# Six places of a decoder layer's schedule moved: fold order, x loads, pool factors, rotary tables, splits behind a copy, an early Exp

## The chip, the cores and the metric

The kernel runs on one core of one Trainium2 chip. The core has TensorE (PE, matmuls into PSUM banks), VectorE (DVE), ScalarE (ACT), GpSimd (POOL) and SyncE (SP, which here only issues transfers), and 16 DMA engines that all transfer queues share. The metric is device time in microseconds (us) of one launch. About 0.2% of it, 4.9 us, is what a measurement of this kernel can tell from no change.

## The reference

One decoder layer in fp32: 2048 tokens, 1024 columns. It is a mixer (retention with rotary tables and a pooling branch, one output projection), cross-attention into 256 memory tokens, and a gated MLP with a short convolution, with a residual after each and a final RMSNorm.

```python
h = rmsnorm(x, mix_norm_g)
q, k, v, gate, u = split(h @ w_in)
mix = concat(head_rmsnorm(retention(rope(q), rope(k), v)) * silu(gate), pool_mixer(u, pool_w, pool_scale))
x = x + mix @ w_out
mem_n = rmsnorm(mem, mem_norm_g)
x = x + cross_attn(rmsnorm(x, xa_norm_g), mem_n, wq, wkv, wo)     # 4 heads, softmax over 256 memory tokens
x = x + conv_glu_ffn(rmsnorm(x, ffn_norm_g), w_up, conv_w, conv_b, w_down)
return rmsnorm(x, final_norm_g)
```

## The kernel before

Every fp32 matmul is made of three passes over pairs. `split` makes a pair: ACT copies the high half (L257, or L260 with a scale), DVE subtracts it from the source to get the low half (L241, or L249 with a scale). `passes` then issues high x high, high x low and low x high (L269, L270, L271). So every operand costs ACT and DVE work ahead of PE, and a low half that is late holds PE at L270 or L271.

**Order.** The engines' instruction orders are made when the kernel is built: a scheduler goes through the program and gives each instruction a place on its engine, with the program's order as priority. `tc.keep_in_program_order` pins an instruction to the program's order on its engine, and `tc.issue_after(x)` keeps instructions behind another. Each engine then runs its list strictly in order: what waits holds all that is behind it.

**Stages.** (1) Start-up, to about 123 us, folds weights: `folded_weights` runs a list of units, K (memory keys, eight), V (memory values, eight), M (score weights: `wq` times keys, evacuated at L552), O (output weights: values times `wo`, L567), W (pool weights: pool factors times `wout_p`, L591). K 1 also starts the memory's norm (sums on PE at L374, copy at L379); odd K units split a pair of keys that the M units need. Between units the caller loads eight tiles of x (`load_x_wide`): a transfer, a scaled split (L260 on ACT, L249 on DVE), a square (L631 on ACT) and an add on DVE (L241), all pinned in order. The list `x_at` tells behind which units. The first W unit also loads the pool factors `poolT`, scales them on DVE and splits them. (2) The value projections, to about 168 us. (3) `head_projections` for the first half of the tokens (b = 0): query, key, gate and pool groups in pairs, each pair as seven block products instead of eight, with sums of blocks made beforehand. Each product fills one PSUM bank; `evac` copies it out (L1668) or adds it, and `final` applies the rotary tables (L1684 on ACT). The tables come back from `rope_d` by four transfers (L1582) and are scaled on DVE in `scaled_tables`, one of the steps that `step()` advances. `settle()` makes the pairs of finished results for the output projection. (4) Output projection and residual, (5) cross-attention from about 455 us on: per tile of 128 tokens a score product, a row maximum on DVE (L893), an Exp on ACT (L897), a transpose on PE (L870). (6) Stages 2 to 5 again for the second half (b = 1, to about 1195 us), and (7) the MLP to the end.

**Weight sums.** Beside stages 2 to 5 POOL makes the sums of weight blocks in HBM (`weight_sums`): copies and accumulating transfers into `Ad`, `Ud` and `Dd`. Its pace is set by tokens: the program calls `next(under[0])` at fixed places, and every `spacing[0]`-th call writes a token on ACT (`halo`, L957) that POOL copies (L958) before it issues that step's transfers (L938, L941). During start-up's last units spacing is 2, in the values 1, in the heads 3 and 7.

The lines that set the order of start-up:

```python
x_at = (2, 4, 6, 8, 10, 12, 18, 19)
for n, _ in enumerate(folded_weights()):
    if n in x_at:
        load_x_wide(x_at.index(n), total)
```

Of the kernel before, what the change touches and what calls it, by code (L numbers as in the profile page):

```python
# [12 lines left out]
ALU = mybir.AluOpType  # L13
# [123 lines left out]
def trunk(ctx, tc, xT, memT, pos, w_qkgu, w_v, wkv, wqT, wo, wout_r, wout_p, poolT, w_up, w_dn, vecs, consts, outT):  # L137
# [285 lines left out]
    def folded_weights():  # L423
# [147 lines left out]

        pool_pair = []

        def pool_weights(g):

            if g == 0:
                raw = new_raw()
                r3 = raw[:, :SUB].rearrange("p (g c) -> p g c", g=4)
                sp.dma_start(r3, poolT.rearrange("g p c -> p g c"))
                pw = prs.take()  # L580
                tt(dve, r3, r3, bcast(pscale, P), ALU.mult)
                split(raw[:, :SUB], pw.r[:, :SUB], pw.r[:, SUB:])
                pool_pair.append(pw)
            pw = pool_pair[0]
            u = row_pair(wout_p[g])
            for nh in range(2):
                ps = mmps()
                lh = [pw.r[:, i * SUB + g * P : i * SUB + (g + 1) * P] for i in range(2)]
                passes(ps, lh, [r[:, nh * SUB : (nh + 1) * SUB] for r in u], True, True)
                t = result()  # L590
                act.activation(t.f, ps, AF.Copy)  # L591
                keep(tiles4(WPd, nh, g), t, 4)
            if g == 3:
                pw.free()
# [4 lines left out]
                r.free()  # L599

        K, V, M, O, W = keys, memory_values, score_weights, output_weights, pool_weights
        for f, *a in ((K, 0), (K, 1), (K, 2), (K, 3), (K, 4), (K, 5), (K, 6), (M, 0), (K, 7), (V, 0), (M, 1), (V, 1), (V, 2), (M, 2),
                      (V, 3), (V, 4), (O, 0), (M, 3), (V, 5), (O, 1), (V, 6), (V, 7), (O, 2), (W, 0), (W, 1), (O, 3), (W, 2), (W, 3),
                      (none_left,)):
            f(*a)
            yield


# [233 lines left out]
    def attention(sums, beside, pace):  # L842
# [31 lines left out]
            e.free()  # L874

        turned.clear()
        mw = [[], []]
        for _ in load_m(0):
            pass
# [674 lines left out]
    def head_projections(b, v, rb, t1, t2, z, got):  # L1554
# [7 lines left out]
        prs.freed.append(len(prs.one))  # L1562
        prs.one.append(Arena(new_s(F32R, 0), 0, 1, T))
        chained.clear()
        todo, ready, mix, gates, outs, tables = [], [], [None] * KT, {}, {}, []

        def place():
# [9 lines left out]
        def scaled_tables():  # L1577
            out = Z.take(2)
            tables.append(out)
            for to, half in ((0, 0), (0, 1), (2, 0), (1, 1)):  # L1580
                p, i = slice(64 * half, 64 * half + 64), min(to, 1)
                sp.dma_start(out.f[p, i * T : (i + 1) * T].rearrange("p (s c) -> p s c", s=NS), rope_d[to].rearrange("(s p) c -> p s c", s=NS))  # L1582
            yield
            yield
            for j in range(KT // 2):
                negated(part_of(z, 1, j), *xpair(j, 1))
                yield
            z.free(2, 2)
            for i in range(2):
                for s in range(NS):  # L1590
                    d = out.f[:, i * T + s * SUB : i * T + (s + 1) * SUB]
                    tt(dve, d, d, rb[s].f[:, :SUB], ALU.mult)
                yield
# [37 lines left out]
        class Heads(Member):  # L1631
# [26 lines left out]
            def evac(self, i, ps):  # L1658
                role, q = ((0, 0), (1, 1), (0, 1), (0, 0), (1, 1), (0, 1), (1, 0))[i]
                d = self.acc[role][q]  # L1660
                if (role, q) == (1, 0):
                    self.final(role, q, d, ps)
                elif (role, q) in self.seen:
                    tt(dve, d, d, ps, ALU.subtract if role else ALU.add)
                    self.final(role, q, d, d)
                else:
                    self.seen.add((role, q))
                    act.activation(d, ps, AF.Copy, scale=-1.0 if role else 1.0)  # L1668

            def final(self, role, q, d, src):  # L1670

# [8 lines left out]
                if kind < 2:  # L1680
                    cs, cols = tables[0], slice(q * SUB, (q + 1) * SUB)
                    c, sn = cs.f[:, cols], cs.f[:, T + q * SUB : T + (q + 1) * SUB]
                    for to, at in ((slice(0, 64), slice(64, 128)), (slice(64, 128), slice(0, 64))):
                        act.activation(side[to], src[at], AF.Copy, scale=1.0 if src is d else -1.0)  # L1684
# [108 lines left out]
        for at, (m, i) in enumerate(items[:own]):  # L1793
# [7 lines left out]
                passes(ps, [pr[:, h, j * P : (j + 1) * P] for h in range(2)], operand(i, j), j == 0 and i in (0, 1, 3), j == KT // 2 - 1, i != 3)  # L1801
            made[at].free()
            m.evac(i, ps)
            fill()
            if at == own - 3:
                for _ in range(5):
# [18 lines left out]
        while todo:  # L1825
            step()
# [105 lines left out]
    for b in range(NB):  # L1932
# [261 lines left out]
```

## Time and profile before

| | |
|---|---|
| median of 3 runs | 2435.37 us (2433.79 to 2436.63) |
| profiled execution | 2434.47 us, span 2432.7 us, mean TensorE clock 0.993 |
| PE busy | 2398.6 us, 99% of the span |
| DVE, ACT, POOL busy | 1737.0, 1347.0, 304.7 us |
| DMA queues' share of 16 engines | q1 49.7%, q0 (POOL's accumulating transfers) 14.7%, q10 3.3% |

A row of the timeline gives start, duration, engine, line, operation and tiles, and in brackets the idle time of the engine before it with what ended it. Names such as `Z`, `R`, `G`, `Q` are buffers that many tiles share. A matmul's duration includes its pipeline; back to back they start 0.227 us apart (128 x 512). A window of a stage has a granted clock of its own, 1.00 in most of the span.

### The profile page before, as it was taken

Reading aid. Unit: us, or ns where it says so; the run is one execution under the profiler, and the core shown is the slowest. Engines: PE = TensorE matmul, PEld = TensorE weight load, DVE = VectorE, ACT = ScalarE, POOL = GpSimd, SP = SyncE. Lnnn points to the kernel's source line nnn. Section 1 sums busy time; section 2 is a strip of 40 time slices with the busy share of each in tenths; the row PEclk is TensorE's granted clock in tenths of the full one; section 3 lists DMA queues with packets and bytes.
Section 4 is the critical chain, followed back from the end, with each engine's and each line's share of the span. In section 5 each row is a group of like instructions: output and inputs, shape, how many; then the busy total and the mean of one; then the engine's idle time right before and its main releaser. Section 6 shows DMA issues by size and latency. Waiting matters only on the chain.

```text
span 2432.7 us, 33367 instructions
## 1 busy us (share of the span) xinstructions
PE 2398.6 (99%) x11232; PEld 2003.4 (82%) x11232; DVE 1737.0 (71%) x2869; ACT 1347.0 (55%) x2457; POOL 304.7 (13%) x484
## 2 busy tenths in 40 slices
PE   8999999999999999999999999999999999999998
PEld 8877888788888888888888888888888888888887
DVE  8646776565767675565788776887677698867875
ACT  7744553344545453334655655765555577666663
POOL 0045554543000000000001010020000000000000
PEclk9999999999999999999999999999999999999999
DMA  8999999989542234375567564755556478758951
GB/s 311 329 290 289 287 284 301 283 215 308 165 116 83 70 120 142 101 285 168 180 211 260 188 203 147 251 191 164 174 156 212 126 241 308 242 185 277 350 176 73
DMA packets 272844, 514.67 MB, mean 212 GB/s; under 512 B 29856, under 2 KB 60960, under 8 KB 272672
## 3 DMA queue, kind: packets, MB, share of 16 engines
q1 hardware_dynamic: 210640, 398.11, 49.7%
q0 software_dynamic: 37376, 86.00, 14.7%
q10 hardware_dynamic: 24656, 28.43, 3.3%
q8 instruction: 88, 1.44, 0.2%
q14 instruction: 84, 0.69, 0.1%
HBM read 410.19 MB, written 188.22 MB: 246 GB/s over the span
## 4 chain that ended last, share of the span: by engine, by line
PE 89%; DMA 4%; DVE 4%; issue 2%; ACT 2%; SPq 0%; DVEq 0%; ACTq 0%
PE mm L269 28%; PE mm L270 27%; PE mm L271 27%; DVE Z L241 1%; PE aux L269 1%; PE aux L271 1%; PE aux L270 1%; PE aux L870 1%; PE aux L777 1%; PE aux L762 1%; DVE Z L249 1%; DMA Z<-rope_d 1%; PE aux L779 1%; PE aux L751 1%; DVE T L241 1%
## 5 line engine op out<-in xcount | busy, mean ns | idle before, releaser
L269 PE MATMUL mm<-G,Q 128*128 128x512 f32 (+1 forms) x1570 | 610.2, 390 | 5.4 <-ACT T L1668 3.0
L271 PE MATMUL mm<-G,Q 128*128 128x512 f32 (+1 forms) x1570 | 608.0, 389 | 6.2 <-DVE Q L241 6.2
L270 PE MATMUL mm<-G,Q 128*128 128x512 f32 (+1 forms) x1442 | 560.4, 389 | 0.2 <-DVE G L249 0.2
L269 PE MATMUL mm<-G,E 128*128 128x512 f32 (+1 forms) x1132 | 430.2, 383 | 2.2 <-ACT G L257 2.0
L270 PE MATMUL mm<-G,E 128*128 128x512 f32 (+1 forms) x1132 | 431.6, 381 | 0.0
L271 PE MATMUL mm<-G,E 128*128 128x512 f32 (+1 forms) x1132 | 429.2, 382 | 1.2 <-DVE E L241 1.2
L269 PEld LDWEIGHTS mm<-G,Q 128*128 128x128 f32 x1570 | 296.3, 189 | 67.3 <-ACT T L1668 3.4
L271 PEld LDWEIGHTS mm<-G,Q 128*128 128x128 f32 x1570 | 296.4, 189 | 66.2 <-DVE Q L241 6.8
L270 PEld LDWEIGHTS mm<-G,Q 128*128 128x128 f32 x1442 | 272.2, 189 | 54.3 <-DVE G L249 0.4
L241 DVE TENSOR_TENSOR Z<-Z,mm 128x512 f32<-128x512 f32 (+1 forms) x322 | 216.3, 676 | 123.3 <-PE mm L271 117.8
L249 DVE SCALAR_TENSOR_TENSOR Z<-Z,vecs 128x1024 f32<-128x1024 f32 x176 | 224.9, 1282 | 50.3 <-ACT Z L1106 47.0
L269 PEld LDWEIGHTS mm<-G,E 128*128 128x128 f32 x1132 | 213.0, 188 | 43.6 <-ACT G L257 2.2
L271 PEld LDWEIGHTS mm<-G,E 128*128 128x128 f32 x1132 | 212.6, 188 | 42.6 <-DVE E L241 1.6
L270 PEld LDWEIGHTS mm<-G,E 128*128 128x128 f32 x1132 | 212.8, 188 | 41.1
L1043 ACT ACTIVATE E<-R 128x512 fp32r<-128x512 f32 (+1 forms) x165 | 101.5, 615 | 140.9 <-PE mm L270 134.9
L241 DVE TENSOR_TENSOR Q<-R,Q 128x512 fp32r<-128x512 f32 (+1 forms) x153 | 106.1, 695 | 65.8 <-ACT Q L257 37.0
L241 DVE TENSOR_TENSOR T<-T 128x512 f32<-128x512 f32 (+4 forms) x196 | 134.7, 692 | 19.9 <-ACT T L416 10.9
L1106 ACT ACTIVATE Z<-Z,vecs 128x1024 f32<-128x1024 f32 x88 | 109.1, 1241 | 42.5 <-DVE Z L241 41.6
L241 DVE TENSOR_TENSOR G<-T,G 128x512 fp32r<-128x512 f32 x165 | 110.4, 691 | 30.8 <-ACT G L990 15.9
L990 ACT ACTIVATE G<-T 128x512 fp32r<-128x512 f32 x180 | 108.2, 623 | 32.7 <-DMA T<-Gd 23.5
L1043 ACT ACTIVATE E<-S 128x512 fp32r<-128x512 f32 (+1 forms) x107 | 65.7, 615 | 102.5 <-PE mm L270 101.0
L241 DVE TENSOR_TENSOR E<-R,E 128x512 fp32r<-128x512 f32 (+2 forms) x127 | 86.5, 683 | 42.9 <-ACT E L1043 42.8
(346 smaller groups left out, 4019.8 us busy)
## 6 DMA issues: line engine op xcount, KB each, us to landing
T<-Gd SPq DMA_DIRECT2D x168, 256.0 KB, 4.4
Ud<-w_up POOLq DMA_DIRECT2D x132, 256.0 KB, 9.9
Gd<-Z SPq DMA_DIRECT2D x110, 256.0 KB, 2.8
R<-Ud SPq DMA_DIRECT2D x106, 256.0 KB, 2.7
R<-w_up SPq DMA_DIRECT2D x80, 256.0 KB, 3.1
S<-Ud SPq DMA_DIRECT2D x70, 256.0 KB, 2.9
Gd<-T SPq DMA_DIRECT2D x56, 256.0 KB, 3.4
T<-Xd SPq DMA_DIRECT2D x53, 256.0 KB, 4.4
```

The costliest lines, as they stand in the source:

```text
L241: return eng.tensor_tensor(out=out, in0=a, in1=b, op=op)
L249: return dve.scalar_tensor_tensor(out=out, in0=a, scalar=s, in1=b, op0=op0, op1=op1)
L269: pe.matmul(ps, lh, rh, start=start, stop=False, skip_group_check=more)
L270: pe.matmul(ps, lh, rl, start=False, stop=False, skip_group_check=more)
L271: latest[0] = pe.matmul(ps, ll, rh, start=False, stop=stop, skip_group_check=more)
L751: pe.matmul(col(sc, c), self.ch(k, c), self.ch(q, c), start=True, stop=True)
L762: pe.matmul(col(kv, c), col(self.kn.f, c), self.ch(v, c, h * T), start=True, stop=True)
L777: pe.matmul(col(y, c), col(self.pr.f, c), self.ch(v, c, h * T), start=True, stop=self.cur[c] is None)
L779: pe.matmul(col(y, c), self.ch(q, c), self.cur[c], start=False, stop=True)
L990: one = act.activation(hi, x, AF.Copy, scale=-1.0 if i == 2 else 1.0)
L1043: act.activation(p2[:, 0, :w], self.raw[i].f[:, :w], AF.Copy)
L1106: act.activation(self.c[g].f, a[:, 2:], AF.Identity, bias=cb[:, f : f + 1], scale=cw[2][:, f : f + 1])
```

## The change

Six edits, in the order of the program. (a) The unit list has K 7, V 0 ahead of M 0, and later units in another order; the first six x tiles are loaded one to three units later. (b) The pool factors have a function of their own, called after M 3. (c) While the values run, the weight sums' spacing goes to 2 once four items are done. (d) For the first half of the tokens four more `yield`s stand ahead of the scaling of the tables. (e) `settle()` is called for every item of the last six, behind the last copy that `evac` or `final` issued on ACT (`read[0]`), and once more at the end. (f) Ahead of attention ACT runs an Exp on two columns.

```diff
+        def pool_factors():
+            raw = new_raw()
...
+            pool_pair.append(pw)
         def pool_weights(g):
-            if g == 0:
-                raw = new_raw()
...
-                pool_pair.append(pw)
...
-        for f, *a in ((K, 0), (K, 1), (K, 2), (K, 3), (K, 4), (K, 5), (K, 6), (M, 0), (K, 7), (V, 0), (M, 1), (V, 1), (V, 2), (M, 2),
-                      (V, 3), (V, 4), (O, 0), (M, 3), (V, 5), (O, 1), (V, 6), (V, 7), (O, 2), (W, 0), (W, 1), (O, 3), (W, 2), (W, 3),
+        for f, *a in ((K, 0), (K, 1), (K, 2), (K, 3), (K, 4), (K, 5), (K, 6), (K, 7), (V, 0), (M, 0), (V, 1), (M, 1), (V, 2), (V, 3),
+                      (M, 2), (O, 0), (V, 4), (M, 3), (V, 5), (V, 6), (O, 1), (V, 7), (O, 2), (W, 0), (W, 1), (O, 3), (W, 2), (W, 3),
                       (none_left,)):
             f(*a)
+            if f is M and a[0] == 3:
+                pool_factors()
...
+        tc.keep_in_program_order(act.activation(halo[:, 39], cs_t[:, P : P + 2], AF.Exp))
...
             z.free(2, 2)
+            if b == 0:
+                for _ in range(4):
+                    yield
             for i in range(2):
...
-                    act.activation(d, ps, AF.Copy, scale=-1.0 if role else 1.0)
+                    read[0] = act.activation(d, ps, AF.Copy, scale=-1.0 if role else 1.0)
...
-                        act.activation(side[to], src[at], AF.Copy, scale=1.0 if src is d else -1.0)
+                        read[0] = act.activation(side[to], src[at], AF.Copy, scale=1.0 if src is d else -1.0)
...
             m.evac(i, ps)
+            with tc.issue_after(read[0].ins):
+                if at > own - 6:
+                    settle()
...
-                with tc.issue_after(chained[-1].ins) if len(chained) == HEADS else nullcontext():
-                    if at >= own - 6:
-                        settle()
...
+        settle()
         finish()
...
-    wv, total, x_at = [], raws.take(), (2, 4, 6, 8, 10, 12, 18, 19)
+    wv, total, x_at = [], raws.take(), (5, 7, 8, 10, 12, 13, 18, 19)
...
-        if n == 21:
+        if n == 22:
             rn = rows_norm([total])
...
             if b == 0:
+                spacing[0] = 2 if place[0] > 3 else 1
                 next(under[0], None)
```

**ACT in start-up, around the memory norm's copy** (T from aux, L379). Splits of weights are L257; x tiles are split by L260 and squared by L631 (L635 after). Before:

```order
L260 ACTIVATE G<-R,vecs 128x1024
L257 ACTIVATE G<-Z_74 128x1024 x2
L631 ACTIVATE R<-R 128x1024
L260 ACTIVATE G<-Z_74,vecs 128x1024
L257 ACTIVATE Q<-Z_74 128x1024
L257 ACTIVATE E_73<-S_78 128x1024
L631 ACTIVATE Z_74<-Z_74 128x1024
L260 ACTIVATE G<-S_79,vecs 128x1024
L257 ACTIVATE G<-R 128x1024
L257 ACTIVATE G<-Z_74 128x1024
L631 ACTIVATE S_79<-S_79 128x1024
L257 ACTIVATE E_73<-R 128x1024
```

and in the changed kernel:

```order
L257 ACTIVATE G<-R 128x1024
L379 ACTIVATE T<-aux_224 128x256
L260 ACTIVATE G<-R,vecs 128x1024
L257 ACTIVATE E_73<-Z_74 128x1024
L257 ACTIVATE G<-T 128x2x256 x3
L260 ACTIVATE G<-R,vecs 128x1024
L257 ACTIVATE G<-T 128x2x256
L260 ACTIVATE G<-S_79,vecs 128x1024
L257 ACTIVATE G<-S_78 128x1024
L635 ACTIVATE R<-R 128x1024
```

The first three x tiles stood ahead of L379, and now none does: all eight stand behind it.

**DVE at the first rotary tables** (`Z<-Z,T`, four scalings; `Q<-R,Q` is the low half of a pair that PE waits for). Before:

```order
L249 SCALAR_TENSOR_TENSOR G<-Z_74,G 128x512
L241 TENSOR_TENSOR G<-Z_74,G 128x512
L241 TENSOR_TENSOR Z_74<-Z_74,T 128x512 x2
L241 TENSOR_TENSOR Q<-R,Q 128x512
L241 TENSOR_TENSOR Z_74<-Z_74,T 128x512 x2
L241 TENSOR_TENSOR Q<-R,Q 128x512
L241 TENSOR_TENSOR E_1670<-E_1670,mm_1743 128x512
```

and in the changed kernel:

```order
L249 SCALAR_TENSOR_TENSOR G<-Z_74,G 128x512
L241 TENSOR_TENSOR G<-Z_74,G 128x512
L241 TENSOR_TENSOR Z_74<-Z_74,T 128x512 x2
L241 TENSOR_TENSOR Q<-R,Q 128x512
L241 TENSOR_TENSOR Z_74<-Z_74,T 128x512 x2
L241 TENSOR_TENSOR Q<-R,Q 128x512
L241 TENSOR_TENSOR E_1623<-E_1623,mm_1693 128x512
```

Nothing moved here.

**ACT near the end of the first heads**, around the copies of one bank (T from mm, L1668; L1677 after). G from Z and G from E are the splits of finished results, Q from R is a weight's high half. Before:

```order
L257 ACTIVATE G<-Z_74 128x512 x4
L1668 ACTIVATE T<-mm_3112 128x512
L1684 ACTIVATE R<-mm_2938 64x512 x2
L257 ACTIVATE G<-E_1670 128x512 x4
L1653 ACTIVATE Q<-R 128x512
L1668 ACTIVATE T<-mm_3112 128x512
```

and in the changed kernel:

```order
L257 ACTIVATE G<-Z_74 128x512 x2
L1677 ACTIVATE T<-mm_3052 128x512
L1693 ACTIVATE R<-mm_2878 64x512 x2
L1662 ACTIVATE Q<-R 128x512
L1677 ACTIVATE T<-mm_3052 128x512
```

Two of the four splits of Z and all four of E moved behind the two copies.

More of the change, by code (lines that the diff above doesn't have):

```diff
@@ L572, in folded_weights @@
         pool_pair = []
-        def pool_weights(g):
-            if g == 0:
-                raw = new_raw()
[L578 to L582, printed above, removed]
-                pool_pair.append(pw)
+        def pool_factors():
+            raw = new_raw()
+            r3 = raw[:, :SUB].rearrange("p (g c) -> p g c", g=4)
+            sp.dma_start(r3, poolT.rearrange("g p c -> p g c"))
+            pw = prs.take()
+            tt(dve, r3, r3, bcast(pscale, P), ALU.mult)
+            split(raw[:, :SUB], pw.r[:, :SUB], pw.r[:, SUB:])
+            pool_pair.append(pw)
+        def pool_weights(g):
             pw = pool_pair[0]
@@ L1564, in head_projections @@
         chained.clear()
+        read = [None]
         todo, ready, mix, gates, outs, tables = [], [], [None] * KT, {}, {}, []
```

## Prediction

> **What bounds the kernel now.** I read the page's busy times first, then TensorE's waits, then windows of the stages that the diff touches, and last the rows around each wait.
>
> ```profile
> PE 2398.6 (99%) x11232; PEld 2003.4 (82%) x11232; DVE 1737.0 (71%) x2869; ACT 1347.0 (55%) x2457; POOL 304.7 (13%) x484
> ```
> ```profile
> PE mm L271 <- DVE Q L241: 6.2, 2, 6.0
> PE mm L269 <- ACT Q L257: 3.7, 3, 2.9
> PE mm L269 <- ACT T L1668: 3.0, 2, 2.3
> PE mm L269 <- ACT G L257: 2.0, 1, 2.0
> PE aux L870 <- DVE T L245: 1.9, 1, 1.9
> PE aux L374 <- DVE Q L241: 1.5, 1, 1.5
> ```
>
> TensorE (PE) is busy 2398.6 of 2432.7 us, so all its idle time is 34.1 us. The matmuls are the same before and after. The change can win only idle time, and matmuls that ran at a slow clock behind it. Each row gives the wait's total, its count and its longest. The six sum to 18.3 us, and the edits are aimed at places where these waits stand: start-up (3.7, 2.0, 1.5), the first rotary tables (6.0 of the 6.2), the end of the heads (3.0), the first Exp (1.9).
>
> Two windows show start-up from 33 us on; columns are length, then busy us (and instructions) of PE, weight loads, DVE, ACT, POOL, then PE's clock, DMA share and GB/s:
>
> ```profile
> 33.00:112.00 79.00, 71.08 (x481) 65.70 (x482) 66.19 (x99) 64.40 (x100) 3.09 (x5) 0.93 0.93 317
> 112.00:123.00 11.00, 11.00 (x38) 8.76 (x38) 4.02 (x5) 6.49 (x10) 0.00 (x0) 0.76 0.72 206
> ```
>
> PE idles 7.9 us in the first; the clock costs about 71.08 x 0.07 = 5.0 there and 11 x 0.24 = 2.6 in the second. At most 15.5 us can be won in start-up. VectorE (DVE) and ScalarE (ACT) are nearly as full, with 12.8 and 14.6 us idle.
>
> **Start-up: keys first, x loads later, pool factors earlier.** ACT's rows show what the first fold and the W units wait for:
>
> ```profile
> 35.02 0.38 ACT L379 ACTIVATE T<-aux 128x256 f32<-128x256 f32 x1 [0.73 <-PE aux L374]
> 36.31 1.83 ACT L257 ACTIVATE G<-T 128x512 fp32r<-128x512 f32 x3 [0.91 <-DVE T L241]
> ...
> 43.91 0.84 ACT L552 ACTIVATE Z<-mm,vecs 128x256 f32<-128x256 f32 x2 [2.23 <-PE mm L271]
> ...
> 105.72 0.63 ACT L257 ACTIVATE Q<-Z 128x512 fp32r<-128x512 f32 x1 [0.76 <-ACT G L257]
> 108.44 1.08 ACT L591 ACTIVATE Z<-mm 128x512 f32<-128x512 f32 x2 [2.08 <-PE mm L271]
> 110.60 1.06 ACT L257 ACTIVATE Q<-Z 128x1024 fp32r<-128x1024 f32 x1 [1.08 <-DMA Z<-wout_p]
> ```
>
> The memory norm (L374, L379) ends late, so the first score fold starts late; at the other end the pool factors are split at 105.72 and wout_p arrives at 110.60. With keys 7, V0 and V1 ahead of the first fold the norm has cover, and the factors move off the W units. These six waits are 7.8 us of ACT's 14.6.
>
> But three x tiles that stood ahead of L379 in ACT's order now stand behind it, and each costs these rows once:
>
> ```profile
> L260 ACT ACTIVATE G<-Z,vecs 128x1024 fp32r<-128x1024 f32 x3 | 3.5, 1166 | 0.0
> L631 ACT ACTIVATE Z<-Z 128x1024 f32<-128x1024 f32 x3 | 3.2, 1068 | 0.0
> ```
> ```profile
> L249 DVE SCALAR_TENSOR_TENSOR G<-Z,vecs,G 128x1024 fp32r<-128x1024 f32 x3 | 3.9, 1287 | 0.2 <-ACT G L260 0.2
> L241 DVE TENSOR_TENSOR R<-R,Z 128x1024 f32<-128x1024 f32 x3 | 3.7, 1221 | 1.1 <-ACT Z L631 1.1
> ```
>
> That is 2.2 us a tile on ACT and 2.5 on DVE: 6.6 and 7.5 us moved out of the data-bound first 33 us into the stretch where both are nearly full. ACT then has 64.4 + 6.6 = 71.0 us of work. If the 7.8 us of waits go and the other 6.8 stay, it reaches the same point 71.0 + 6.8 = 77.8 us after 33, against 79.0: 1.2 us won. DVE has 66.2 + 7.5 = 73.7 and so needs its idle cut from 12.8 to about 5. If in addition W1 starts without the long wait, the slow clock of the second window (2.6) goes: 3.8. I take -3.0. The bounds are -15.5 (all idle and slow time gone) and, if ACT keeps all its 14.6 us of idle, 71.0 + 14.6 - 79 = +6.6.
>
> On what stalls cost in clock, after the 2.88-us wait at 111.71 the matmuls stood 0.43 us apart:
>
> ```profile
> 113.15 0.63 PE L270 MATMUL mm<-G 128*128 128x512 f32 x1
> 113.58 0.63 PE L271 MATMUL mm<-G 128*128 128x512 f32 x1
> ```
>
> The Trainium skill ("TensorE: Matmul & The Clock Gate", Part 1: The HAM clock gate) says that the array falls to half rate after an idle window of about 3.4 us and needs about as long of work to recover. This trace is harsher: shorter waits in a row were enough here. The rule speaks against the change where it puts waits for V2's or V6's split on PE: with two such windows, each 3.4 us at half rate, my estimate from the page is +3.4, and start-up would win nothing.
>
> **The first rotary tables: tables later, fewer weight sums.** The biggest single wait is this chain:
>
> ```profile
> 169.90 13.93 DMA Z<-rope_d
> 184.05 0.51 issue
> 184.56 0.68 DVE Z L241
> 185.25 0.61 DVE Q L241
> 185.91 0.79 PE mm L271
> ```
>
> DVE waits for rope_d to scale the tables, and a split's low half (Q, L241), which PE needs, is queued behind. Two edits bear on it. Four more yields ahead of the scaling would let the low half pass; but DVE's order has the same rows at this place in both kernels (front, second place), so this edit moves nothing here: 0. The other thins the weight sums that POOL starts beside the values. Their transfers share the DMA engines, which are full (the last two figures are share and GB/s):
>
> ```profile
> 180.00:190.00 10.00, 4.09 (x12) 0.66 1.06 303
> ```
>
> Here I counted tokens. POOL takes a step when ACT has written a token (L957) and POOL has copied it (L958); up to 168 us:
>
> ```profile
> L957 ACT ACTIVATE halo<-consts x20: 182/190/218, 89.9 to 165.9; 128x2 f32<-128x2 f32 x20
> L958 POOL COPY halo<-halo x11: 187/476/1483, 90.2 to 167.8; 128x2 f32<-128x2 f32 x11
> ```
>
> ACT is nine tokens ahead of POOL. The edit cuts the 20 tokens to 14, which is still ahead of the eleventh copy, and POOL's order has 46 transfers ahead of the fourteenth copy where it had 45. So up to about 186 us POOL would start the same transfers at the same pace, rope_d would land as late, and the wait stays. I take 0; the bounds are -7.4 (the 6.0 us, and for the slow matmuls behind it 4.09 busy us x 0.34 of clock = 1.4) and +1.4, a tenth more on the 13.93-us transfer if an earlier start crowds it.
>
> **End of the heads: the bank's copy first.** ACT's rows, then PE's:
>
> ```profile
> 341.36 2.23 ACT L257 ACTIVATE G<-Z 128x512 fp32r<-128x512 f32 x4
> 343.44 0.64 ACT L1668 ACTIVATE T<-mm 128x512 f32<-128x512 f32 x1
> 344.10 1.20 ACT L1684 ACTIVATE R<-mm 64x512 f32<-64x512 f32 x2
> 345.32 2.19 ACT L257 ACTIVATE G<-E 128x512 fp32r<-128x512 f32 x4
> 347.42 0.61 ACT L1653 ACTIVATE Q<-R 128x512 fp32r<-128x512 f32 x1
> ```
> ```profile
> 344.13 0.50 PE L269 MATMUL mm<-G,Q 128*128 128x512 f32 x1 [2.32 <-ACT T L1668]
> 348.09 0.50 PE L269 MATMUL mm<-G,Q 128*128 128x512 f32 x1 [0.92 <-ACT Q L1653]
> ```
>
> In the new order two of the four splits G<-Z stand ahead of the copy T<-mm instead of four: at (343.44 - 341.36) / 4 = 0.52 us each, the copy starts 1.04 us earlier. The four splits G<-E go behind Q<-R, which then ends near 345, ahead of PE's need: 0.92 gone. Together -2.0 (bounds -3.2, both waits gone, and 0, if the copy then waits for the matmuls of its own bank). The moved splits hide under the twelve matmuls between these two rows and those behind; uncovered, they would cost their 2.19. In the second half the like place is smaller:
>
> ```profile
> 859.00 0.50 PE L269 MATMUL mm<-G,Q 128*128 128x512 f32 x1 [0.67 <-ACT T L1668]
> ```
>
> Two splits of 0.52 leave the copy's front, more than the 0.67: -0.5 (0 to -0.7).
>
> **Exp's table ahead of attention.**
>
> ```profile
> 476.04 1.28 ACT L897 ACT_TABLE_LOAD   x1 [17.60 <-issue]
> 477.34 0.57 ACT L897 ACTIVATE T<-mm,sm,scl 128x256 f32<-128x256 f32 x1
> ```
> ```profile
> 479.18 0.70 PE L870 MATMUL aux<-consts,T 128*128 128x128 f32 x4 [1.90 <-DVE T L245]
> ```
>
> ACT idles 17.60 us, then loads the table only once its first real Exp may run; PE's wait follows. The new tiny Exp pulls the load into that idle time: -1.3, the load's own length, leaving 0.6 of PE's wait. Bounds 0 (the load not on the path) and -1.9. The Trainium skill ("ScalarE: Activation LUTs", What ACT_TABLE_LOAD costs) gives 1.28 us for a load and some 1.38 us of drain besides; by that the term would be the whole 1.9. The trace agrees on the load, while its Exp starts 0.02 us behind it, with no drain to win. At the second attention PE shows no wait, so nothing is won there.
>
> **Sum.** -3.0 + 0 - 2.0 - 0.5 - 1.3 = -6.8. From the profiled execution, 2434.47 us (span 2432.7 and 1.8 around it), that is 2427.7; the median, 2435.37, lies 0.9 above it, so against it I say 2428.6.
>
> **Rivals.** *The tables' wait goes too*: if fewer sums do thin the queues before rope_d is issued, 7.4 more are won: 2421.2. For: DMA is full there and rope_d took 13.93 us. Against: the nine tokens of lead. *Start-up clears*: ACT and DVE follow and PE loses nothing from 33 us on: -15.5 - 3.8 = -19.3, 2416.1. For: the first fold's and the W units' waits are those removed. Against: 73.7 us of DVE work in 79. *Start-up gives nothing*: the waits move to V2's or V6's splits behind the x tiles, 0 to +3 there: 2431.6 to 2434.6, no change. *Slower*: DVE becomes the bound of start-up. Its price is its whole old idle kept on top of the moved tiles, 73.7 + 12.8 - 79 = +7.5, and a second stretch of slow matmuls like the one of 2.6: +10.1 - 3.8 = +6.3, 2441.7. It decides once W1 starts later than about 120 us (8.7 after the 111.71 of now, where the 3.8 are spent and 4.9 lost); for it speaks that lows on DVE release PE, against it that half of DVE's idle was waiting for ACT work that is removed. *The change doesn't do what it says* holds already for the tables' four steps.
>
> **How the numbers follow.** Forecast 0.42, own range 2424 to 2432; tables too 0.15; start-up clears 0.12; nothing at start-up 0.18; slower 0.13. About 0.2%, 4.9 us, is what a measurement of this kernel can tell from no change, so faster means under 2430.5. Three quarters of the forecast and both gaining rivals: 0.31 + 0.15 + 0.12 = 0.58. The rest of the forecast and the empty start-up: 0.29. Slower 0.13. For 8 in 10 the range leaves out the far end of the cleared start-up and most of the slower case: 2415 to 2438.
>
> **What would show it.** In the profile after: no wait of aux L374 near 34 us and the first M matmuls near 50; W1 at about 108 to 110 and without its wait for wout_p; the 6-us wait on DVE Q with its 13-us rope_d transfer still there, shifted by what start-up won; the waits at 344 at 1.3 and 0; the table load near 458 and PE's wait at the first aux L870 near 0.6. I am wrong if rope_d lands before PE gets there, if POOL's eleventh copy comes later than now relative to the values, or if the values start later than now.

## The result: slower by half a per cent, and the profile after

The changed kernel takes 2448.91 us (median of 4 runs, 2445.5 to 2449.71), beside 2436.0 us of the kernel before in the same session (2433.79 to 2437.59). The ratio is 1.0051, with a 95% interval of 1.0034 to 1.0068: slower. The forecast was 2428.6 us, in a range that ended at 2438. The profiled execution, the fastest of the four, has a span of 2443.7 us, 11.0 more than before. One execution among all that follow, of the last kernel, took 11010.75 us and is left out of that kernel's figures.

The page of the changed kernel gives the busy times; TensorE's waits follow (total, count, longest).

```profile
PE 2401.8 (98%) x11232; PEld 2006.5 (82%) x11232; DVE 1733.2 (71%) x2869; ACT 1347.8 (55%) x2459; POOL 311.0 (13%) x484
```
```profile
PE mm L269 <- ACT G L257: 6.9, 2, 5.5
PE mm L269 <- ACT E L257: 6.5, 1, 6.5
PE aux L350 <- DVE R L241: 5.7, 1, 5.7
PE mm L271 <- DVE Q L241: 5.2, 2, 4.9
PE mm L269 <- ACT T L1677: 3.4, 2, 2.1
PE aux L874 <- DVE T L245: 0.6, 1, 0.6
```

The work is the same (DVE and ACT within 4 us of before). The list of waits is another one: the three at its top, 19.1 us, all lie in start-up, where the same three had at most 2.0 us each before. To set places against each other I added up, row by row, how much later PE's matmuls start than back to back at full clock; below this is called the loss of a stretch. It puts the 11.0 us like this:

| stretch | loss before | loss after |
|---|---|---|
| start-up, 30 to 130 us | 15.8 | 28.4 |
| first rotary tables | 7.7 | 7.2 |
| end of the heads, first half | 3.8 | 2.1 |
| first Exp | 2.5 | 1.2 |
| end of the heads, second half | 2.3 | 4.0 |

All but start-up moves by 1.7 us or less. Start-up itself I divided once more, with 0.227 us (128 x 512) and 0.120 us (128 x 256) as back to back, which adds 0.3 and 0.7 us to its two sums:

| stretch | loss before | loss after |
|---|---|---|
| 30 to 62 us | 7.3 | 7.4 |
| 62 to 100 us | 0.2 | 10.4 |
| 100 to 130 us | 8.6 | 11.3 |

Up to 62 us the change loses no more than the kernel before; most of the difference comes behind that. In start-up the windows of the two kernels part at 30 us (columns as in the prediction: length, busy of PE, weight loads, DVE, ACT, POOL, then clock, DMA share, GB/s). The kernel before, and then the changed one:

```profile
30.00:40.00 10.00, 6.53 (x38) 5.78 (x37) 9.83 (x21) 5.63 (x9) 0.00 (x0) 0.77 0.94 366
50.00:60.00 10.00, 9.78 (x80) 9.52 (x79) 9.52 (x13) 9.15 (x16) 0.00 (x0) 1.00 0.92 304
```
```profile
30.00:40.00 10.00, 9.92 (x83) 9.71 (x82) 8.87 (x12) 9.03 (x12) 0.00 (x0) 1.00 0.59 192
50.00:60.00 10.00, 4.51 (x27) 4.31 (x26) 9.17 (x12) 6.63 (x10) 0.00 (x0) 0.83 1.00 341
90.00:100.00 10.00, 9.23 (x46) 8.62 (x47) 4.87 (x5) 5.47 (x8) 0.00 (x0) 0.66 0.91 305
120.00:130.00 10.00, 8.50 (x30) 6.39 (x30) 5.03 (x17) 4.11 (x5) 0.00 (x0) 0.62 0.79 293
```

From 30 to 40 us PE does well after the change, since it has keys to fold, but the transfers fall from a share of 0.94 to 0.59. PE pays for that in the fifties (4.51 busy of 10). From 40 to 50 us the share is low in both (0.47 and 0.56).

**Why the transfers stop.** SyncE's issues of the two kernels in this stretch, before and then after (`x2` with a long duration is two issues with a wait between them):

```profile
25.07 4.54 SPq L466 DMA_DIRECT2D Z<-wqT  x2
30.49 0.33 SPq L340 DMA_DIRECT2D S<-wkv  x1
31.63 0.33 SPq L340 DMA_DIRECT2D R<-wkv  x1
32.01 0.42 SPq L629 DMA_DIRECT2D R<-xT  x1
32.83 3.20 SPq L340 DMA_DIRECT2D Z<-wkv  x2
41.38 0.33 SPq L466 DMA_DIRECT2D R<-wqT  x1
```
```profile
29.77 3.01 SPq L466 DMA_DIRECT2D Z<-wqT  x2
38.32 0.33 SPq L466 DMA_DIRECT2D Z<-wo  x1
44.59 5.33 SPq L340 DMA_DIRECT2D S<-wkv  x2
```

Between 25 and 44 us the kernel before issues seven weights and an x tile, the changed one three weights. Weights and x tiles share ten load places (three in `R`, two `S`, five in `Z`), one of which keeps the running sum of squares, from the first x tile on. A place is free again when its last reader is done. For the other x tiles that is the square on ACT (L631, L635 after) and its addition on DVE.

No x tile is squared before 40.4 us, where the first square ran at 16.9. The data did not come that much later: the first four tiles landed at 12.9, 16.8, 23.0 and 28.1 us before, and at 17.1, 24.0, 29.1 and 31.7 after, since SyncE loads ahead as far as places allow. The second to fourth tile, which hold places of their own, waited 24.8 us together from landing to square before, and 52.5 us after. ACT's rows of the changed kernel show what they stood behind:

```profile
32.98 0.39 ACT L379 ACTIVATE T<-aux 128x256 f32<-128x256 f32 x1 [0.86 <-PE aux L374]
33.27 1.14 ACT L260 ACTIVATE G<-R,vecs 128x1024 fp32r<-128x1024 f32 x1
36.82 1.14 ACT L260 ACTIVATE G<-R,vecs 128x1024 fp32r<-128x1024 f32 x1
```

A pinned instruction stands behind the one that the program gives its engine just before it; pinned ones are not all held in order with each other. The addresses in the program tell the tiles apart: the split at 33.27 is the third tile's, 1.6 us after its data, and the first tile's is the one at 36.82, 19.8 us after its data. The second's follows at 38.38. The first two tiles are now loaded behind K 5 and K 7, odd units that split a pair of keys, and those splits need the norm's copy at 32.98. Before, these tiles stood behind K 2 and K 4.

The number of places held is not what differs: from 32 to 47 us three x tiles hold places of their own in both kernels. What differs is which load waits for them. SyncE issues in order, and its issues at 44.59 and 49.59 us (the second of the `x2`) came 0.03 us behind the ends of these two rows of DVE:

```profile
43.34 1.22 DVE L241 TENSOR_TENSOR G<-S,G 128x1024 fp32r<-128x1024 f32 x1
48.33 1.23 DVE L241 TENSOR_TENSOR R<-R,S 128x1024 f32<-128x1024 f32 x1
```

The first is the low half of a weight. The second adds the second x tile, which had landed at 24.0 us. All other loads stood behind these two: an `R` place that was done with at 33.57 us got its next load at 49.97.

**Then three stalls.** PE's rows, each with the wait in brackets:

```profile
56.40 0.58 PE L269 MATMUL mm<-G 128*128 128x256 f32 x1 [5.49 <-ACT G L257]
90.30 0.58 PE L269 MATMUL mm<-G,E 128*128 128x256 f32 x1 [6.49 <-ACT E L257]
119.26 3.57 PE L350 MATMUL aux<-consts,R 128*128 128x1 f32 x16 [5.75 <-DVE R L241]
```

The first is V 2: its weight was issued at 49.59 us, into the second x tile's place, and landed at 55.3, and ACT split it at once. It costs no more than the early waits of before that are gone (7.4 and 7.3 us up to 62). The second carries most of the net loss. It is ACT, whose results go out from `Z` and hold its order until their transfers have read them:

```profile
82.34 1.21 ACT L552 ACTIVATE Z<-mm,vecs 128x256 f32<-128x256 f32 x3 [2.57 <-DMA Md<-Z]
86.52 0.84 ACT L552 ACTIVATE Z<-mm,vecs 128x256 f32<-128x256 f32 x2 [2.61 <-DMA VWd<-Z]
87.38 1.28 ACT L693 ACT_TABLE_LOAD   x1
89.21 1.04 ACT L257 ACTIVATE E<-Z 128x1024 fp32r<-128x1024 f32 x1
```

In the chain of waits that result's transfer took 9.67 us, while late weights were being loaded on the same engines; that these are why it took so long is not shown. The third is the sum of squares, which waits for the x tiles: the last to land came at 85.4 us and was squared at 113.4, where the last landing was at 75.8 before and the last square at 100.4. The slow clock behind the stalls is part of the loss: in the windows above, busy time by the share of clock that is missing, 4.51 x 0.17 + 9.23 x 0.34 + 8.50 x 0.38 = 7.1 us. The Trainium skill ("TensorE: Matmul & The Clock Gate", Part 1: The HAM clock gate) has the array fall to half rate after an idle window of about 3.4 us; the rows agree for these three waits, which are all longer: behind the first, matmuls of 128 x 256 start 0.21 us apart for 2.3 us, and then 0.12.

### The profile page after: what moved, and what is told of

The parts are those of the page before. It is cut to its first block, busy times and chain, and to the rows that moved or that the text cites. A ratio compares the mean times of both kernels' runs of the same rounds, so it can differ in the third digit from the quotient of the medians.

```text
span 2443.7 us, 33379 instructions
## 1 busy us (share of the span) xinstructions
PE 2401.8 (98%) x11232; PEld 2006.5 (82%) x11232; DVE 1733.2 (71%) x2869; ACT 1347.8 (55%) x2459; POOL 311.0 (13%) x484
## 4 chain that ended last, share of the span: by engine, by line
PE 91%; DMA 4%; DVE 2%; ACT 2%; issue 1%; SPq 0%; ACTq 0%; DVEq 0%
PE mm L269 28%; PE mm L271 28%; PE mm L270 28%; PE aux L269 1%; PE aux L271 1%; PE aux L270 1%; PE aux L755 1%; PE aux L874 1%; PE aux L781 1%; PE aux L766 1%; DMA Z<-rope_d 1%; DVE Z L241 1%; PE aux L783 1%; DMA R<-xT 0%; DMA VWd<-Z 0%
## 5 line engine op out<-in xcount | busy, mean ns | idle before, releaser
L269 PEld LDWEIGHTS mm<-G,E 128*128 128x128 f32 x1140 | 216.0, 190 | 47.8 <-ACT E L257 6.7
L271 PEld LDWEIGHTS mm<-G,E 128*128 128x128 f32 x1140 | 215.4, 189 | 43.3 <-DVE E L241 2.3
L270 PEld LDWEIGHTS mm<-G,E 128*128 128x128 f32 x1140 | 216.1, 190 | 41.1
```

The lines of the kernel that those rows point to most:

```text
L269: pe.matmul(ps, lh, rh, start=start, stop=False, skip_group_check=more)
L270: pe.matmul(ps, lh, rl, start=False, stop=False, skip_group_check=more)
L271: latest[0] = pe.matmul(ps, ll, rh, start=False, stop=stop, skip_group_check=more)
```

## The experiments

Each was timed beside the kernel before on the same chip; ratios are against that, with 95% intervals. In the first round theory A blamed the later x loads and theory B the new list of units.

**Start-up put back.** The changed kernel with the old list, the old x loads and the pool factors in the first W unit:

```diff
-    ... x_at = (5, 7, 8, 10, 12, 13, 18, 19)
+    ... x_at = (2, 4, 6, 8, 10, 12, 18, 19)
+    (the list of units, `n == 21` and the pool factors as before)
```

> The changed kernel with the start-up of before (old unit order, old x loads, pool factors back in the first W unit); the other four edits stay. If the whole loss is start-up's, as the two traces say (PE's idle and slow time from 30 to 130 us grew by about 12.5 us, the rest of the span fell by about 1.5), this runs 1 to 3 us faster than before, near 2434. Rival: the later edits disturb transfers in the second half and take their part of the loss; then it stays 4 us or more above before.

2435.26 against 2434.38 us: 0.9995 (0.9986 to 1.0004), no change. The loss is in start-up. The gain of 1 to 3 us did not come. In the profiled execution, which was the slowest of the eleven (2439.45 us), a wait had grown elsewhere, at the start of attention: PE's first transpose, then the DVE instruction ahead of it:

```profile
481.65 1.12 PE L870 MATMUL aux<-consts,T 128*128 128x128 f32 x4 [5.56 <-DVE T L245]
```
```profile
475.13 0.49 DVE L245 TENSOR_SCALAR T<-T,consts 128x512 f32<-128x512 int32 x1 [13.90 <-DMA T<-pos]
```

The load of the positions took 7.7 us here (5.9 before), and DVE, in order, took the row maxima of attention after it. So Exp's table, early as it was, won nothing in this run.

**The list of units alone**, on the kernel before:

```diff
-        ... (K, 6), (M, 0), (K, 7), (V, 0), (M, 1), ...
+        ... (K, 6), (K, 7), (V, 0), (M, 0), (V, 1), (M, 1), ...
```

> Before with only the new unit list. Theory A (the x tiles, which come later and hold load buffers longer, starve the weight loads; the unit list is innocent): within 3 us of before. Theory B (the unit list itself: five V and O units in a row need buffers for results and for weights faster than stores and loads free them): 6 us or more slower, with a wait for a split of V2 or a later V unit of 4 us or more.

2429.69 us, 0.998 (0.9972 to 0.9989): 4.9 us faster. Theory B falls. But the new order does not clear start-up: the first fold's waits come back two units later.

```profile
44.69 1.19 PE L269 MATMUL mm<-G 128*128 128x256 f32 x4 [3.48 <-ACT G L257]
48.35 0.58 PE L270 MATMUL mm<-G 128*128 128x256 f32 x1 [2.23 <-DVE G L241]
```

The gain is at the tables, where waits of 1.26, 1.23 and 0.77 stand in place of one of 5.98, though `rope_d` still took 9.6 to 14.5 us.

**The late x loads alone**, on the kernel before:

```diff
-    ... x_at = (2, 4, 6, 8, 10, 12, 18, 19)
+    ... x_at = (5, 7, 8, 10, 12, 13, 18, 19)
```

> Before with only the later x loads. Theory A: 6 us or more slower, with weight loads issued late between 35 and 55 us. Theory B: within 3 us of before, perhaps a little faster, since keys 6 and 7 get their loads sooner.

2443.6 us, 1.0036 (1.0024 to 1.0049): 9.2 us slower, from this line alone. The row for 33 to 112 us, to be set beside the prediction's (71.08 of PE, 0.93 of DMA):

```profile
33.00:112.00 79.00, 67.75 (x456) 62.67 (x454) 62.98 (x77) 63.55 (x97) 2.84 (x5) 0.94 0.83 274
```

PE, DVE, ACT and the transfers all have less to do. Over this stretch none of the engines has become the bound. As in the change, the loss lies behind 62 us: from 62 to 100 us it is 12.7 us, where the kernel before loses 0.2.

**The pool factors alone**, on the kernel before:

```diff
+            if f is M and a[0] == 3:
+                pool_factors()
```

> Before with only the pool factors moved behind M 3. By my forecast's step the first W units lose their waits of 1.1, 0.5 and 2.9 us and part of the slow clock behind: 2 to 5 us faster. Rival (theory C: the factors take a load buffer and a transfer in a stretch that has none to spare): no change or slower, the wait for wout_p stays.

2434.12 us, 0.9994 (0.9985 to 1.0002): no change. The W units' waits of 1.07, 0.48 and 2.88 us became 0.86, 0.47, 1.49 and 1.72, now for banks that ACT copies (L593, L567). The even time hides two changes: start-up loses some 3 us more, and the tables' wait of 5.98 is down to 2.60, with one of 0.78 behind it.

**The changed kernel with the old x loads**:

```diff
-    ... x_at = (5, 7, 8, 10, 12, 13, 18, 19)
+    ... x_at = (2, 4, 6, 8, 10, 12, 18, 19)
```

> The changed kernel with the x loads back where they were; new unit order and all other edits stay. If the later x loads are the whole cause, also in company of the new unit order, this runs 5 to 8 us faster than before (the unit list alone won 4.9, and the head and Exp edits add a little). Rival: the new unit order loses too once the pool factors and the sums' pace are changed with it; then 0 to 6 us slower than before.

2425.46 us, 0.9969 (0.9957 to 0.998): 9.1 us faster than before, and some 20 faster than the change as it was made (1.0051 less 0.9969 is 0.8%). The loss of 30 to 130 us is back at 15.6, of which 62 to 100 us has 0.1. So the new list wins nothing in start-up itself; the gain is the tables' wait, of which 0.26 us is left. DVE's rows show why:

```profile
172.33 0.69 DVE L241 TENSOR_TENSOR Q<-R,Q 128x512 fp32r<-128x512 f32 x1 [5.99 <-ACT Q L1662]
176.91 1.29 DVE L241 TENSOR_TENSOR Z<-Z,T 128x512 f32<-128x512 f32 x2 [3.89 <-DMA Z<-rope_d]
178.12 0.68 DVE L241 TENSOR_TENSOR Q<-R,Q 128x512 fp32r<-128x512 f32 x1
```

One low half (`Q<-R,Q`) now stands ahead of the first scaling (`Z<-Z,T`); before, and in the changed kernel, both stood behind scalings. `rope_d` still took 10.1 to 13.4 us, but what PE needs no longer queues behind it.

**The late x loads, unpinned.** The changed kernel, with the x tiles' split, square and addition free to take another place in ACT's and DVE's order:

```diff
-        split(f, X[:, 2 * k], X[:, 2 * k + 1], mixg[:, k : k + 1], kept="both")
-        tc.keep_in_program_order(act.activation(f, f, AF.Square))
+        split(f, X[:, 2 * k], X[:, 2 * k + 1], mixg[:, k : k + 1])
+        act.activation(f, f, AF.Square)
```

(and the same for the addition)

> The changed kernel whose x tiles' split, square and sum are not pinned in program order on ScalarE and VectorE, so that they may be placed in the idle time between 20 and 33 us, when the first tiles have landed; the list of x loads stays late. Theory H (held places: tiles that land at 17 to 32 us and are worked on from 40 us on keep load places from the weights): half of the loss or more goes, 6 us or more faster than the changed kernel. Rival (the order of the transfers, or the work itself moved late): within 3 us of the changed kernel, and the DMA share between 30 and 50 us stays near 0.6.

2434.06 us, 1.0001 (0.9992 to 1.001): some 13 us better than the change, with the late list as it was. The scheduler puts the first tile's split where its data come, at 17 us instead of 37:

```profile
17.15 1.15 ACT L260 ACTIVATE G<-R,vecs 128x1024 fp32r<-128x1024 f32 x1 [0.17 <-DMA R<-xT]
```

The second to fourth tile wait 15.2 us together from landing to square, where it was 52.5. The second tile's addition ends at 28.5, and V 2's weight goes into its place 21 us earlier than in the change:

```profile
28.52 0.33 SPq L340 DMA_DIRECT2D S<-wkv  x1
```

The wait at 56.40 does not come. By parts the loss is 10.1, 3.4 and 3.9 us (7.4, 10.4 and 11.3 in the change), so what this wins comes behind 62 us. The reason isn't that DVE has less to do: from 31 to 54 us its rows for x tiles take 9.8 us here, 8.6 in the change and 3.8 before. So it isn't the late place in the program as such that costs, but that it pins the work on tiles that are there already.

**One load place fewer**, on the kernel before:

```diff
-    raws = Places(... + [(Z.t, j * T) for j in range(5)], T)
+    raws = Places(... + [(Z.t, j * T) for j in range(4)], T)
```

> Before with one load place less in start-up (nine instead of ten). Theory H, where start-up is bound by free load places: 3 us or more slower, with a lower DMA share from 33 to 112 us. Rival (places are no limit, the engines' work is): within 1.5 us of before.

2436.2 us, 1.0009 (1.0 to 1.0018). The time misses what was expected of it, but the place is seen at work: PE does 116.14 us of work up to 136 us, where it was 124.68, and a wait of 10 us appears.

```profile
121.45 2.07 PE L269 MATMUL mm<-G 128*128 128x512 f32 x4 [10.04 <-ACT G L257]
```

The tables' wait then falls from 5.98 to 0.56, and start-up's loss is taken up there.

**More yields ahead of the scaling**, on the kernel before, twelve of them (its first query and key rotations then use tables that are not scaled yet, so a part of the computation differs):

```diff
+            if b == 0:
+                for _ in range(12):
+                    yield
```

> Before with twelve yields ahead of the tables' scaling instead of four: at twelve VectorE's order does change, the low halves and bank sums go ahead of the scaling that waits for rope_d. If the 6.0-us wait comes from the order on VectorE alone, it goes, with the slow matmuls behind it: 5 to 7.5 us faster than before. Rival: the wait only moves to the first use of the tables (the heads' finals) or to a bank whose copy is late: less than 3 us faster.

2438.05 us, 1.0013 (1.0005 to 1.0022). With the change's four steps DVE's order stayed as it was; with twelve it differs, and PE is busy in all of 160 to 200 us (34.02 before). The wait comes back 190 us later, in the same half's heads:

```profile
375.84 0.47 PE L792 MATMUL aux<-consts,T 128*128 128x128 f32 x1 [6.02 <-ACT T L787]
```

Together with three others of 0.75 to 1.62 us, nothing is left of the gain.

**Only the first four x loads early**, on the changed kernel:

```diff
-    ... x_at = (5, 7, 8, 10, 12, 13, 18, 19)
+    ... x_at = (2, 4, 6, 8, 12, 13, 18, 19)
```

> The changed kernel with only the first four x loads back where they were; tiles 5 and 6 stay later, and all else of the change. Theory H2 (the first four tiles, which land by 32 us and are then worked on from 40 us on, are the loss): within 3 us of the kernel with all x loads back, about 6 to 9 us faster than before. Rival (it is the later tiles, whose square and sum end late and hold PE's sum of squares ahead of the W units): half of the loss or more stays, 0 to 6 us slower than before.

2431.78 us, 0.9991 (0.9982 to 0.9999). From +12.9 us to -2.5: these four carry most of it. Some 6 us to the kernel with all loads early remain, as waits of 1.06 and 1.74 near 126 us and 2.28 for the positions' load at 474.64.

**A pace that binds**, on the kernel before: from the second item of the values on, POOL's steps are spaced by eight calls.

```diff
+                spacing[0] = 8 if place[0] > 0 else 1
```

> Before with the weight sums' spacing at 8 from the second item of the values on, so that tokens, not POOL, set the pace. My forecast's counting says that the cut to 14 tokens did nothing because POOL was behind its tokens. If so, a cut that does bind shortens rope_d's transfers from 10.7 to 13.9 us to about 3 to 6 and takes most of the 6.0-us wait: 4 to 7 us faster. Rival: the queue is filled by SyncE's own loads, rope_d takes 9 us or more as before; or the sums are then late for the heads, and a wait for an Ad load comes instead.

2425.04 us, 0.9963 (0.995 to 0.9975): 9.3 us faster with one line. POOL has made seven copies by 168 us, where it had made eleven, and the transfers have room:

```profile
L958 POOL COPY halo<-halo x7: 185/902/1146, 89.0 to 166.4; 128x2 f32<-128x2 f32 x7
```
```profile
150.00:190.00 40.00, 40.00 (x178) 33.15 (x177) 27.15 (x48) 20.10 (x38) 13.49 (x20) 1.00 0.80 228
```

The DMA share of this window was 1.06 before. `rope_d` takes 6.9 to 8.3 us instead of up to 13.9, and the wait is gone. The Trainium skill ("DMA: Bandwidth & Descriptors", Issuing engines are not separate DMA queues) says that transfers interleave on the same 16 engines whichever engine issued them; these rows agree.

**Splits behind the copy for the first half only**, on the changed kernel with the old x loads:

```diff
-            with tc.issue_after(read[0].ins):
-                if at > own - 6:
-                    settle()
+            if b == 0:
+                with tc.issue_after(read[0].ins):
+                    if at > own - 6:
+                        settle()
```

(and the old place of `settle()` for the second half)

> The changed kernel with all x loads back, and the results' splits behind the bank's copy only in the first half of the tokens; in the second half they stand as before. The second half's wait near 850 us should return from 1.9 us to the 1.1 and 0.7 of before, so no more than 1 us is to be had over the kernel with the x loads back: about 0.3% faster than before.

2427.85 us, 0.9974 (0.9963 to 0.9986). In the second half the waits are back at 1.07 and 0.68, as expected. The kernel is no better than the one with the old x loads alone: other waits came in (1.47 and 0.77 at the tables, 1.73 for the positions, 2.34 at a W unit).

**Places held, order kept**, on the kernel before: the places of the second to fourth x tile are given back only behind the 13th unit.

```diff
+            if k < 4:
+                held.append(r)
+            else:
+                r.free()
...
+        if n == 12:
+            for r in held:
+                r.free()
```

> Before with the load places of the second to fourth x tile kept from other loads until the thirteenth unit; no work is moved by the program. Theory H (places held by x tiles starve the weight loads): DMA share from 33 to 60 us falls by 0.1 or more, and PE's busy time to 136 us by 3 us or more; 2 to 8 us slower. Rival (places are no limit, the order of the pinned work is): PE's busy time to 136 us within 1.5 us of before.

2438.65 us, 1.0016 (1.0007 to 1.0025): 4.3 us slower. Holding places costs time with ACT's and DVE's order of x tiles unchanged, and W 1 is late again:

```profile
117.90 1.22 PE L269 MATMUL mm<-Q 128*128 128x512 f32 x2 [3.76 <-ACT Q L257]
```

But the DMA share of 33 to 60 us is 0.75 as before, and not lower as expected; it falls later (0.89 for 33 to 112, from 0.93). So the run shows that held places cost time, but not by the shortage that was expected.

**The binding pace with the new units, and with the old ones.** The changed kernel with the old x loads and spacing 8; and the same with the old units and pool factors:

```diff
-    ... x_at = (5, 7, 8, 10, 12, 13, 18, 19)
+    ... x_at = (2, 4, 6, 8, 10, 12, 18, 19)
-                spacing[0] = 2 if place[0] > 3 else 1
+                spacing[0] = 8 if place[0] > 0 else 1
```

> The changed kernel with all x loads back and the weight sums' spacing at 8 in the values, so that the tables' wait is out of the way: new unit order, pool factors early, splits behind the copy, early Exp. If the forecast's -3 for start-up's unit order was right, this is about 3 us faster than the like kernel with the old order, near 2419 where before is 2434.5. If the order only shifts start-up's waits and won its 4.9 us at the tables, the two are within 1.5 us.

> The same with the unit order, x loads and pool factors of before: the thinner sums (9 us faster alone), the splits behind the copy in both halves (about -0.5 in sum) and the early Exp (-1.3): 10 to 11 us faster than before, near 2424. Rival: the gains do not add, since the tables' wait hid others: 9 us or less.

2424.84 us, 0.9962 (0.995 to 0.9974), and 2426.0 us, 0.9969 (0.9957 to 0.9982). The intervals overlap: once the tables' wait is gone, a gain of the new units is not shown (loss of 30 to 130 us 16.5 and 15.5). Nor do gains add: the old x loads in the changed kernel, the pace alone, and both together all end near 2425. In both of these runs the positions' load is late (waits of 2.55 and 3.58 us at 469).

Up to 136 us the kernels compare like this; PE's busy time up to there, and the DMA share from 30 to 40 us:

| kernel | PE busy to 136 us | DMA share, 30 to 40 | against before, us |
|---|---|---|---|
| before | 124.68 | 0.94 | |
| old x loads in the changed kernel | 122.61 | 0.92 | -9.1 |
| late loads, unpinned | 122.03 | 0.84 | -0.5 |
| late loads alone | 117.28 | 0.63 | +9.2 |
| the change | 112.86 | 0.59 | +12.9 |

## Why the prediction was wrong, step by step

**Start-up, -3.0 (bounds -15.5 to +6.6): the step that failed.** It measured +12.6. The step counted what the later x loads move as work, 2.2 us of ACT and 2.5 of DVE a tile, and asked whether the two engines have room for it. Over 33 to 112 us they had: DVE did 58.88 us and ACT 61.03 in the changed kernel, less than the 66.19 and 64.40 of before. (DVE had none from 31 to 54 us, 22.79 us busy of 23, but that was so before as well.) What it left out is what waits for the tiles' places meanwhile. It took the loads to come later with the units; SyncE issues them as soon as places allow, and only their readers came later. The upper bound was a bound for ACT's idle time alone, so it had no room for this. What the runs showed in its place: the late loads by themselves cost 9.2 us, taking them back wins 20 in the changed kernel, letting their readers go early wins 13 with the loads late, and fewer or held places cost PE 8.5 and 3.5 us of work up to 136 us. The first stall is traced to one held place. How the second and third, which make the net loss, follow from the late loads is not settled: letting the readers go early moves the work as well as the holds, and holding three places alone, with the x tiles' order kept, cost 4.3. That the late loads cost 9 with the old list of units and 20 with the new one comes in part from the tables: of the 20, start-up is 12.8 (28.4 against 15.6) and the first tables 6.6 (7.2 against 0.6).

**The sources named for that gain.** The norm's wait at L374 did go, and PE was full to 50 us. But with early x loads the new list has the same loss as the old (15.6 and 15.8): its cover is used up and the waits come at 44 and 48 us. The pool factors won nothing, as the W units wait for the banks' copies next. So even without the x loads the -3.0 was not there; what the list won, it won at the tables.

**The rivals.** The slower case had the right sign, and its point of decision, W 1 later than about 120 us, was met (split at 126.5). Its mechanism was another: it made DVE's work from 33 to 112 us the bound, and DVE did less there. *Start-up gives nothing* is what happens with the old x loads.

**The rotary tables, 0.** Right for this kernel, for the reasons given: in the same order, a `rope_d` as long as before and PE's wait 4.94 us (5.98 before).

```profile
182.61 13.68 DMA Z<-rope_d
```
```profile
198.36 0.79 PE L271 MATMUL mm<-G,Q 128*128 128x512 f32 x1 [4.94 <-DVE Q L241]
```

The count of tokens held too: 14 tokens did not bind (POOL made nine copies by 172 us), eight calls a step did, and won 9.3 us. The rival that the wait goes came true as soon as the x loads were undone, and by another way than fewer sums: one low half ahead of the scalings.

**End of the heads, -2.0 and -0.5.** PE's rows in the changed kernel:

```profile
356.15 0.50 PE L269 MATMUL mm<-G,Q 128*128 128x512 f32 x1 [1.29 <-ACT T L1677]
```
```profile
868.05 0.63 PE L269 MATMUL mm<-G,Q 128*128 128x512 f32 x1 [2.14 <-ACT T L1677]
```

First half: 1.29 was forecast as 1.3, and the second wait is gone (one of 0.26 us for DVE stands near its place); the loss fell by 1.7. Second half: 2.14 where 0.1 was forecast. The step looked at ACT's copy alone and missed what PE does while it waits. In the kernel before, eight transposes stood there:

```profile
857.16 1.16 PE L751 MATMUL aux<-Z 128*128 128x128 f32 x8 [1.07 <-DVE E L249]
859.00 0.50 PE L269 MATMUL mm<-G,Q 128*128 128x512 f32 x1 [0.67 <-ACT T L1668]
```

In the changed kernel they run at 872.50, behind the copy. Counted from PE's instruction ahead of both (855.06 and 864.87), the product starts after 3.94 us before and 3.18 after: the copy is 0.8 us earlier, but the eight transposes (1.16 us) that had filled the time are still to be done. The next matmuls then start 0.43 us apart, eight of them, where they started 0.23 apart; that makes most of the 1.7 us by which the loss grew. With the old place of `settle()` there, the transposes were back ahead and the waits 1.07 and 0.68.

**Exp's table, -1.3.** Right: the table is loaded in ACT's idle time, and PE waits 0.63 us where 1.90 stood (forecast 0.6).

```profile
469.47 1.28 ACT L881 ACT_TABLE_LOAD   x1
487.07 0.56 ACT L902 ACTIVATE T<-mm,sm,scl 128x256 f32<-128x256 f32 x1 [16.11 <-DVE sm L245]
```

But ACT now waits for the row maximum on DVE, and in six other runs that was late behind the positions' load. The 1.3 us are not safe.

## What to carry to other kernels

When a load is moved in a program that loads ahead, ask when its last reader runs: what lands early and is read late holds a place, and with loads issued in order the one that waits for that place holds back all behind it (here the second x tile, 24 us after its landing, set when V 2's weight was loaded). Thinning a background stream does nothing until the pace binds, so count how far ahead its tokens are; and with an in-order engine, look at what queues behind a waiting instruction before shortening the transfer that it waits for. Parts of a change should be undone one by one: without the later x loads this one is 9.1 us faster than before, and with them 12.9 us slower.

## What was not expected of the hardware

The loads of the positions (`T<-pos`) took 5.4 to 8.7 us in all kernels but one (2.9 and 3.0 us with the pace that binds and the rest as before), though none of them touches these loads. In kernels with the early Exp it moved PE's wait at the start of attention between 0.54 and 5.56 us, some 350 us behind the edits.

A stall can be taken up elsewhere: 8.5 us less of PE's work in start-up became 2 at the end with nine places, since the tables' wait swallowed the rest. It can also come back: 6.02 us at 376 for 5.98 at 185 with twelve yields.

One wait of 2.14 us at 868.05 was followed by 3.4 us of matmuls 0.43 us apart. In the kernel before, waits of 1.07 and 0.67 at the same place were followed by matmuls 0.23 us apart, and 1.29 us at 356.15 cost no clock either.
